# A hybrid encoder layer on one core: front steps in another order, joint level operands, 64-row products of two heads in turn

## The chip, the cores and the metric

The kernel runs on one core of one Trainium2 chip. The metric is the device time of one execution in microseconds (us), taken as the median of the runs. Engines carry the names of the profile: PE does the matmuls, DVE the vector work, ACT activations, copies and casts, POOL some vector work and the gathers by index, and SP issues most transfers. A line such as L656 is a line of the kernel's code.

## The reference, cut to what matters

One encoder layer over 512 tokens and 16 meta tokens of width 1024, in float32: a differential attention group and a bidirectional gated linear attention (GLA) group side by side, an output projection, and then a feed-forward part (PEER) in which each token picks its experts out of 16384.

```
xn = rmsnorm(h);  dq,dk,dv, gq,gk,gv,gr, zf,zb = split(xn @ w_in)
da = diff_attention(dq, dk, dv)             # 4 heads, 2 x 64 wide, values 128 wide
go = gla(gq, gk, gv, log_sigmoid gates)     # 4 heads, 64-wide keys, forward + backward
h  = h + concat(rmsnorm(da), rmsnorm(go) * silu(gr)) @ w_out
hn = rmsnorm(h)
s  = (hn @ w_q) . sub_keys                  # 8 heads x 2 halves x 128 keys
idx, gate = top 16 of the 16 x 16 sums of both halves' top 16
h  = h + sum_k gate * gelu(hn . u[idx]) * v[idx]
```

The output is the final RMSNorm of h without the meta tokens.

## The kernel before

All large products are exact to about float32: each operand is split into a rounded part (hi) and a rest (lo), and three matmuls, hi·hi (L131), lo·hi (L132) and hi·lo (L133), add up in one PSUM bank. ACT casts hi (L118 for streamed weights, L138 for other operands), and DVE or POOL subtracts to get lo (L120, L139).

The program has three parts.

**Front.** All projections, both attention groups and `w_out`. The string `ORDER` (L69) gives the order in which the code emits steps: `v`, `k`, `q` are projections of the attention group, `x` the GLA keys and queries of the second pair of heads, `u` one attention unit (16 of them: 4 heads by 4 blocks of queries), `w` one of the eight column blocks of `w_out` (`wo_pass`, `wo_first`), and `G` and `g` one step of the generator `gla_pair` for the first and second pair of heads. A GLA pair has twelve steps: seven levels, one that projects `gv` and `gr`, two for the chunk states (forward, backward), and two that finish one head each. In a level, DVE and POOL subtract prefix sums of the gates (`pre`; L672 and L673 on DVE), ACT takes exp, DVE multiplies with queries and keys (L677, L678: tile `ef`), PE multiplies 64-row operands (`pairmm`, L656: head 0 sits in rows 0 to 63, head 1 in rows 64 to 127, four chunks of 128 tokens each) and DVE writes the masked result into `AT` (L681). The last two steps make, per head and chunk, one product of `AT` with the values (L751) and two products of the queries with the states (`qx`·`S`, L753 and L754, again 64 rows).

**Middle.** The queries of PEER (`wq`, 16 blocks of 24 matmuls), the product with the keys (L953), and then the choice of the top 16 on DVE (`top16`, `topk2`: L188 to L256), which ends for the first 128 tokens with the tile `idx` (L992). `iof` (L922) and `keys` (L924) are loaded by SP. While DVE works on this, PE goes on with `u_tile`s (below).

**Experts.** For tokens 128 to 511 every expert is computed: 128 U tiles (`u_tile`: 24 matmuls of 384 columns, then gelu) and 128 V tiles (`v_tile`: 18 matmuls of 512 columns, tile weights `vhl`). U tiles 0 to 59 run alone, their results go to memory (`A_d`); from then on U and V tiles alternate. The gate weights for the V tiles are made as outer products of one-hot tiles (`oh`, L1024 and L1029 on DVE; L1060 and L1063 on PE, 96 banks of eight matmuls), which are placed among the U tiles: bank group n belongs to tile `A0 + int(n * AR)`, plus `AG` from n = `AL` on. The first 128 tokens use their chosen experts alone: POOL gathers a row of u or v per token (L264, 128 times each), DVE multiplies it with the token (L278) or adds it to the sum (L276). `pull(r)` hands out gathers in shares: `RA` per tile from tile `GS0` to 49, `RV` and `RUV` per V tile after that; a gather also waits until the tile three before is done.

The code emits in this order, and a scheduler that simulates the engines then sets the order of instructions on each engine; it may move independent work past each other.

## Time and profile before

| | us |
|---|---|
| median of three runs | 1642.83 |
| the runs | 1638.16, 1642.83, 1642.96 |
| profiled execution, its own time | 1635.18 |
| span of the profiled execution, first to last instruction | 1633.4 |
| PE busy (96% of the span) | 1561.7 |
| DVE busy (77%) | 1261.5 |
| ACT busy (44%) | 712.7 |
| POOL busy (35%) | 563.7 |
| mean granted TensorE clock, share of full | 0.985 |

The profile is of one execution, which took 7.65 us less than the median of the three runs. PE is busy in nearly all of it, so the questions to ask are where PE still waits, and where it is busy at less than its pace: on products that leave half of the array unused, or at a lower granted clock. A count behind an x is a count of records; a float32 matmul has two of them, a split one (L131 to L133) has one.

### The profile page before, as it was taken

To read this page: it belongs to the slowest core of one execution; us is meant where nothing else is said; L and a number is where in the kernel's file an instruction comes from. 1 tells how busy PE (TensorE), PEld (TensorE's weight loads), DVE (VectorE), ACT (ScalarE), POOL (GpSimd) and SP (SyncE) were. 2 spreads that over 40 slices of the span, in tenths; PEclk is the share of its full clock that TensorE was granted. 3 is DMA by queue.
4 is the path that set the end of the run, shared out by engine and by line. 5 is a ranking of instruction groups with operands and counts; after the bars stand their busy time and mean duration, and the time that the engine had idled before them with its cause. 6 is when DMAs were issued, how large, how long until landed. Compare 5 with 4: busy or idle time off the path is not lost.

```text
span 1633.4 us, 24035 instructions
## 1 busy us (share of the span) xinstructions
PE 1561.7 (96%) x8793; PEld 1382.3 (85%) x8793; DVE 1261.5 (77%) x2492; ACT 712.7 (44%) x1131; POOL 563.7 (35%) x419
## 2 busy tenths in 40 slices
PE   6999999999997789999999999999999999999997
PEld 6887886778897788989888888889999999998886
DVE  3888767655999796977467787788878887787877
ACT  5444654544332466777343333333333333333333
POOL 3445113048553330040011112265454443444442
PEclk9999999999999899999999999999999999999999
DMA  7112212233233466778999998799999999999975
GB/s 235 59 48 83 66 55 69 84 104 118 79 133 112 133 235 241 296 265 304 375 350 323 319 315 312 272 369 360 324 348 330 330 338 318 329 353 328 331 252 193
DMA packets 152358, 387.40 MB, mean 237 GB/s; under 512 B 12752, under 2 KB 71376, under 8 KB 150576
## 3 DMA queue, kind: packets, MB, share of 16 engines
q1 hardware_dynamic: 104432, 213.62, 38.0%
q0 software_dynamic: 36864, 134.23, 23.2%
q10 hardware_dynamic: 10944, 38.02, 6.2%
q8 instruction: 69, 1.13, 0.3%
q14 instruction: 49, 0.40, 0.1%
HBM read 342.56 MB, written 40.63 MB: 235 GB/s over the span
## 4 chain that ended last, share of the span: by engine, by line
PE 46%; issue 19%; DVE 15%; DMA 10%; POOL 7%; ACT 2%; SPq 1%; POOLq 0%; ACTq 0%; DVEq 0%
POOL gat L264 7%; PE bankg L131 6%; PE bankg L133 6%; PE bankg L132 6%; PE banka L1119 5%; PE banka L1122 5%; PE banka L1123 5%; DMA gat<-v,idx 4%; DMA gat<-u,idx 3%; PE bankp L1123 2%; PE bankp L1122 2%; PE bankp L1119 2%; DVE tiv L192 1%; DVE tiv L189 1%; DVE sc L190 1%
## 5 line engine op out<-in xcount | busy, mean ns | idle before, releaser
L264 POOL DMA_INDIRECT gat<-u,idx x128 | 201.6, 1575 | 531.2 <-PE bankp L1123 251.6
L118 ACT CAST hi<-raw 128x1024 fp32r<-128x1024 f32 x177 | 185.8, 1051 | 320.3 <-PE bankg L132 191.1
L131 PE MATMUL bankg<-un_hi,hi 128*128 128x384 f32 x896 | 303.4, 339 | 3.9 <-ACT act L1094 3.9
L132 PE MATMUL bankg<-un_lo,hi 128*128 128x384 f32 x896 | 302.5, 338 | 0.0
L133 PE MATMUL bankg<-un_hi,lo 128*128 128x384 f32 x896 | 302.3, 338 | 0.0
L264 POOL DMA_INDIRECT gat<-v,idx x128 | 157.7, 1232 | 206.7 <-PE bankp L1123 172.7
L120 DVE TENSOR_TENSOR lo<-raw,hi 128x1024 fp32r<-128x1024 f32 x142 | 174.0, 1227 | 56.3 <-ACT hi L118 52.4
L276 DVE SCALAR_TENSOR_TENSOR acc<-gat,sact,acc 128x1024 f32<-128x1024 f32 x128 | 164.3, 1284 | 58.1 <-DMA gat<-v,idx 55.0
L278 DVE CUSTOM_DVE_ANT_0 gat<-gat,hn 128x1024 f32<-128x1024 f32 x128 | 155.1, 1219 | 36.8 <-DMA gat<-u,idx 36.1
L139 DVE TENSOR_TENSOR vhl<-vraw,vhl 128x1024 fp32r<-128x1024 f32 x128 | 156.1, 1220 | 27.6 <-ACT vhl L138 26.5
L131 PEld LDWEIGHTS bankg<-un_hi,hi 128*128 128x128 f32 x896 | 169.6, 189 | 7.9 <-ACT act L1094 4.2
L132 PEld LDWEIGHTS bankg<-un_lo,hi 128*128 128x128 f32 x896 | 169.5, 189 | 3.3
L133 PEld LDWEIGHTS bankg<-un_hi,lo 128*128 128x128 f32 x896 | 169.6, 189 | 1.7 <-DVE lo L120 0.2
L138 ACT CAST vhl<-vraw 128x1024 fp32r<-128x1024 f32 x128 | 134.2, 1049 | 55.8 <-PE bankp L1123 34.6
L120 POOL TENSOR_TENSOR lo<-raw,hi 128x1024 fp32r<-128x1024 f32 x35 | 87.1, 2491 | 73.7 <-ACT hi L118 70.1
L1065 ACT ACTIVATE stg<-banka 128x512 f32<-128x512 f32 x96 | 96.9, 1165 | 11.4 <-PE banka L1063 11.0
L1094 ACT ACTIVATE act<-bankg 128x384 f32<-128x384 f32 x112 | 54.5, 487 | 30.2 <-PE bankg L133 20.7
L133 PE MATMUL bankp<-un_hi,lo 128*128 128x384 f32 x128 | 44.6, 348 | 21.9 <-DVE lo L120 21.9
L1024 DVE TENSOR_TENSOR oh<-iT,ioh 128x2048 f16<-128x2048 f16 x48 | 57.5, 1219 | 1.3 <-PE banka L1063 1.3
L1029 DVE TENSOR_TENSOR oh<-oh,gs 128x2048 f16<-128x2048 f16 x48 | 57.7, 1218 | 0.0
L1060 PE MATMUL banka<-oh 128*128 128x128 f16 x384 | 49.5, 221 | 8.2 <-DVE oh L1029 7.3
L1063 PE MATMUL banka<-oh 128*128 128x128 f16 x384 | 49.1, 220 | 0.0
(2287 smaller groups left out, 3775.1 us busy)
## 6 DMA issues: line engine op xcount, KB each, us to landing
raw<-uT SPq DMA_DIRECT2D x128, 512.0 KB
vraw<-v SPq DMA_DIRECT2D x128, 512.0 KB
W_d<-stg ACTq DMA_DIRECT2D x12, 2048.0 KB
wa<-W_d SPq DMA_DIRECT2D x32, 768.0 KB
A_d<-act ACTq DMA_DIRECT2D x60, 192.0 KB
wa<-A_d SPq DMA_DIRECT2D x15, 768.0 KB
raw<-wq SPq DMA_DIRECT2D x16, 512.0 KB
raw<-win_n SPq DMA_DIRECT2D x12, 512.0 KB
```

Of the source, the lines that this page charges most:

```text
L118: nc.scalar.copy(hi, raw)
L120: (eng or nc.vector).tensor_sub(lo, raw, hi.bitcast(F32))
L131: nc.tensor.matmul(o, lhsT=ah, rhs=bh, start=start, stop=False)
L132: nc.tensor.matmul(o, lhsT=ah, rhs=bl, start=False, stop=False)
L133: return nc.tensor.matmul(o, lhsT=al, rhs=bh, start=False, stop=stop)
L138: last[0] = nc.scalar.copy(hi, src).ins.name
L139: (eng or nc.vector).tensor_sub(lo, src, hi.bitcast(F32))
L264: g = nc.gpsimd.indirect_dma_start(out=r, out_offset=None, in_=src, in_offset=bass.IndirectOffsetOnAxis(ap=idx[:, hk:hk + 1], axis=0))
L276: nc.vector.scalar_tensor_tensor(acc0, r, sact[:, hk:hk + 1], acc0, op0=ALU.mult, op1=ALU.add)
L278: nc.vector.tensor_tensor_reduce(r, r, hn0, scale=1.0, scalar=0.0, op0=ALU.mult, op1=ALU.add, accum_out=sact[:, hk:hk + 1])
L1119: m0 = nc.tensor.matmul(o, lhsT=gh_[:, tc_], rhs=vh[:, dc], start=(j == 0), stop=False, skip_group_check=True)
L1122: nc.tensor.matmul(o, lhsT=gh_[:, tc_], rhs=vl[:, dc], start=False, stop=False, skip_group_check=True)
```

## The change

In the front, `ORDER` is a new string: it puts projections (`x`, `v`, `k`, `q`) between the first levels, and `u`, `q`, `k` between the last GLA steps and the first blocks of `w_out`. The GLA queries and keys of a pair lie in one tile `gqk`, and both prefix sums in one tile `pre` (`Bi`, `Fi`), so that a level takes one subtraction on DVE of 512 columns where two of 256 stood, and one multiplication of 1024 where two of 512 stood. POOL's two subtractions stay. `pairmm` takes the two heads in turn within a chunk, each head with a bank of its own. The finish of a pair makes the `AT` products of both heads first and then the `qx`·`S` products, heads in turn. `dg` of the middle and `hT` lie in other buffers. The load of `keys` stands behind the loop that makes `un_hi`, and so the code's order of the two loads on SP changes. Of the numbers, `GS0`, `RA`, `RUV`, `A0` and `AR` change: fewer gathers among the U tiles, more per V tile, and outer products from an earlier tile on. The number of PE matmuls is the same.

```diff
-GS0 = 12
+GS0 = 20
-RA = 0.3
+RA = 0.15
 RV = 0.85
-RUV = 2.92
+RUV = 3.0
-ORDER = 'GGGxGGGGGGGkGGggvgqggukugguqugguuukuvgqgukqgwuwuuuwwwuuuww'
+ORDER = 'GGxGGvGkGGGqGGGGggugkugguqguguvgkuguqgugkuguqwuwuwuwuwuwuww'
-A0 = 15
-AR = 0.48
+A0 = 11
+AR = 0.56
...
-        def pairmm(q_, k_, hh):
-            rows = slice(64 * hh, 64 * hh + 64)
-            b = bank((P, 4, P), tag=PT["pair"])
+        def pairmm(qk):
+            bs = [bank((P, 4, P), tag=PT["pair"]) for _ in range(2)]
             for c in range(4):
                 cs = slice(c * P, (c + 1) * P)
-                nc.tensor.matmul(b[:, c, :], lhsT=k_[rows, cs], rhs=q_[rows, cs], start=True, stop=True)
-            return b
+                for hh in range(2):
+                    rows = slice(64 * hh, 64 * hh + 64)
+                    nc.tensor.matmul(bs[hh][:, c, :], lhsT=qk[rows, 1, cs], rhs=qk[rows, 0, cs], start=True, stop=True)
+            return bs
...
-            nc.vector.tensor_sub(E[:, :, :, 1, :], vf[:, :, :, 1, :], fm)
-            nc.vector.tensor_sub(E[:, :, :, 0, :], bm_, vb[:, :, :, 0, :])
+            nc.vector.tensor_sub(E, fr[:, :, :, 0, :], md.to_broadcast([P, 2, nb, s]))
...
             nc.scalar.activation(ef, ef, AF.Exp, scale=1.0 / 16.0)
-            nc.vector.tensor_mul(ef[:, 0, :], ef[:, 0, :], gq[pair])
-            nc.vector.tensor_mul(ef[:, 1, :], ef[:, 1, :], gk[pair][:, :T])
-            for hh in range(2):
-                b = pairmm(ef[:, 0, :], ef[:, 1, :], hh)
+            nc.vector.tensor_mul(ef, ef, gqk[:, :, :T])
+            for hh, b in enumerate(pairmm(ef)):
                 nc.vector.copy_predicated(AT[hh], msk[:, li, None, :].to_broadcast([P, 4, P]), b)
...
+        gob = [bank((P, 4, P), tag=PT["go"]) for _ in range(2)]
+        for hh in range(2):
+            for c in range(4):
+                nc.tensor.matmul(gob[hh][:, c, :], lhsT=AT[hh][:, c, :], rhs=gv[:, c, hh * P:hh * P + P], start=(c == 0),
+                                 stop=False, skip_group_check=True)
+        for dr in (1, 0):
+            for c in range(3 + (dr == 0)):
+                cs = slice(c * P, c * P + P)
+                for hh in range(2):
+                    r = slice(64 * hh, 64 * hh + 64)
+                    nc.tensor.matmul(gob[hh][:, c, :], lhsT=qx[dr][r, cs], rhs=st[dr][r, c, :], start=False,
+                                     stop=(dr == 0 and c == 3), skip_group_check=True)
         for hh in range(2):
...
-            b = bank((P, 4, P), tag=PT["go"])
-            for c in range(4):
-                cs = slice(c * P, c * P + P)
-                nc.tensor.matmul(b[:, c, :], lhsT=AT[hh][:, c, :], rhs=gv[:, c, hc], start=True, stop=False)
-                if c < 3:
-                    nc.tensor.matmul(b[:, c, :], lhsT=qx[1][r, cs], rhs=st[1][r, c, :], start=False, stop=False)
-                nc.tensor.matmul(b[:, c, :], lhsT=qx[0][r, cs], rhs=st[0][r, c, :], start=False, stop=True)
...
-    dg = tz("dg", [P, 4, P])
+    dg = fx("dgh", [P, 4, P], "gvs")
...
-    keys = qs.tile([P, 2 * PH, NK], F32, name="keys")
-    nc.sync.dma_start(out=keys, in_=I["keys"])
...
         split(un_hi[:, k, :], un_lo[:, k, :], hk, nc.gpsimd)
+    keys = qs.tile([P, 2 * PH, NK], F32, name="keys")
+    nc.sync.dma_start(out=keys, in_=I["keys"])
```

**The products of a level on PE.** Before, with buffer numbers: the four matmuls of head 0 (one bank), then the four of head 1 (the next bank), between split matmuls of a projection.

```order
L132 MATMUL bankg_838<-lo_623,act_hi0_77 128x256
L133 MATMUL bankg_838<-hi_621,act_lo0_79 128x256
L131 MATMUL bankg_838<-hi_680,act_hi1_78 128x256
L656 MATMUL banka_718<-ef_710 128x128 x4
L656 MATMUL banka_724<-ef_710 128x128 x4
L132 MATMUL bankg_838<-lo_682,act_hi1_78 128x256
L133 MATMUL bankg_838<-hi_680,act_lo1_80 128x256
```

After, one level (now L662) of the changed program:

```order
L132 MATMUL bankg_733<-lo_599,act_hi0_77 128x256
L133 MATMUL bankg_733<-hi_597,act_lo0_79 128x256
L662 MATMUL banka_564<-ef_558 128x128
L662 MATMUL banka_565<-ef_558 128x128
L662 MATMUL banka_564<-ef_558 128x128
L662 MATMUL banka_565<-ef_558 128x128
L662 MATMUL banka_564<-ef_558 128x128
L662 MATMUL banka_565<-ef_558 128x128
L662 MATMUL banka_564<-ef_558 128x128
L662 MATMUL banka_565<-ef_558 128x128
```

Each matmul now stands beside one of the other head, in the other half of the rows. The `qx`·`S` products of the second pair stand in turn only in part, and those of the first pair still stand as seven of head 0 and seven of head 1, although the code emits them in turn: the scheduler has drawn them apart.

**The first product with the keys on PE.** Before, the end of 40 `wq` matmuls that stand between the product that makes `hrow` (L903) and the first product with the keys:

```order
L131 MATMUL banka<-hg_hi_3647,hi 128x512
L132 MATMUL banka<-hg_lo_3648,hi 128x512
L133 MATMUL banka<-hg_hi_3647,lo 128x512
L131 MATMUL banka<-hg_hi_3647,hi 128x512
L953 MATMUL bankg<-keys,pq 128x128 x4
L132 MATMUL banka<-hg_lo_3648,hi 128x512
```

After, the same place (L914 makes `hrow` out of `dgh`, L964 is the product with the keys):

```order
L914 MATMUL banka<-dgh,ones 128x512
L131 MATMUL banka<-hg_hi_3473,hi 128x512
L132 MATMUL banka<-hg_lo_3474,hi 128x512
L131 MATMUL banka<-hg_hi_3473,hi 128x512
L132 MATMUL banka<-hg_lo_3474,hi 128x512
L964 MATMUL bankg<-keys,pq 128x128 x4
L133 MATMUL banka<-hg_hi_3473,lo 128x512
```

Four `wq` matmuls stand between the two instead of 40; the later products with the keys follow at the same distance as before. On SP, `keys` now stands ahead of `iof`.

**DVE behind `idx`.** Before, five small operations of the later top-k (the choice for tokens 128 to 511), then the lo parts of the next three U tiles:

```order
L992 SCALAR_TENSOR_TENSOR idx<-sel 128x128
L220 TENSOR_SCALAR sm_row<-sm_bp 128x128
L221 TENSOR_SCALAR sm_bp<-sm_bp 128x128
L226 CAST sm_rf<-sm_row 128x128
L227 CAST sm_cf<-sm_bp 128x128
L229 SCALAR_TENSOR_TENSOR sm_t_6141<-sm_rf,sm_cf 128x128
L120 TENSOR_TENSOR lo<-raw,hi 128x1024 x3
```

After, thirteen such operations stand behind `idx`, of which these are the last three ahead of the first lo part, and what comes before the second:

```order
L239 TENSOR_TENSOR eq<-sm_cb,io16b 128x2048
L212 TENSOR_TENSOR sm_gate<-sm_gate,hrs 128x128
L227 CAST sm_cf<-sm_bp 128x128
L120 TENSOR_TENSOR lo<-raw,hi 128x1024
L231 TENSOR_SCALAR sm_bsv<-sm_rf 128x128
L243 TENSOR_TENSOR eq<-eq,tf 128x2048
L229 SCALAR_TENSOR_TENSOR sm_t_6005<-sm_rf,sm_cf 128x128
L1021 CAST gs<-gT 128x16x8
L1035 TENSOR_TENSOR oh<-iT,ioh 128x2048 x4
L245 TENSOR_TENSOR eq<-eq 128x64x16
L120 TENSOR_TENSOR lo<-raw,hi 128x1024
```

The lo parts that PE waits for moved behind top-k work and behind the first one-hot tiles. The first outer product stands behind U tile 16 instead of 19, the last ahead of tile 49 instead of 52, and the first V tile behind tile 54 instead of 57: six U tiles lie between the last outer product and the first V tile in both.

## Rows read from the trace of the kernel before

**Rows 1.** Busy time by stage: window, then engines, clock, DMA share, GB/s
```profile
0.00:200.00 200.00, 182.47 (x1291) 158.08 (x1292) 146.54 (x311) 105.11 (x210) 76.61 (x84) 0.99 0.30 96
...
460.00:565.00 105.00, 85.25 (x478) 84.71 (x478) 99.31 (x431) 32.09 (x46) 42.14 (x14) 0.90 0.39 130
565.00:797.00 232.00, 214.72 (x1699) 206.80 (x1699) 177.41 (x190) 154.33 (x183) 42.81 (x10) 0.98 0.76 273
797.00:1616.00 819.00, 817.78 (x4000) 723.86 (x3999) 645.95 (x810) 289.25 (x396) 305.50 (x245) 1.00 0.92 325
```
**Rows 2.** What PE waited for, 40 to 355: us in total, times, longest
```profile
PE bankp L471 <- DVE ss L144: 2.0, 1, 2.0
PE banka L769 <- DVE gy L765: 1.9, 1, 1.9
...
PE banka L656 <- DVE ef L678: 0.2, 1, 0.2
```
**Rows 3.** Timeline of PE at one level: start, us, operation, idle before
```profile
73.91 1.68 PE L656 MATMUL banka<-ef 64*128 64x128 f32 x16 [0.25 <-DVE ef L678]
75.52 0.38 PE L132 MATMUL bankg<-lo,act_hi 128*128 128x256 f32 x1
```
**Rows 4.** Line 656 alone, in two windows of 10 ns: records under way
```profile
74.25:74.26 0.01, 0.01 (x3) 0.01 (x2) 1.00 0.00 0
74.57:74.58 0.01, 0.01 (x4) 0.01 (x4) 1.00 0.00 0
```
**Rows 5.** Timeline of PE in the finish of one head
```profile
248.59 0.48 PE L753 MATMUL banka<-S,qx 64*128 64x128 f32 x2
...
249.65 0.48 PE L753 MATMUL banka<-S,qx 64*128 64x128 f32 x2
...
252.18 0.44 PE L538 MATMUL bankp<-ident,dy 128*128 128x128 f32 x2
```
**Rows 6.** Timeline of PE at the end of the second pair
```profile
274.17 0.63 PE L515 MATMUL banka<-ident,pr 128*128 128x128 f32 x4
274.63 0.27 PE L516 MATMUL banka<-ident,pr 128*32 128x128 f32 x1
```
**Rows 7.** Busy time by stage, behind the end of the second pair
```profile
280.00:300.00 20.00, 20.00 (x71) 13.13 (x69) 11.97 (x31) 11.41 (x39) 0.00 (x0) 0.68 0.17 53
```
**Rows 8.** What SP's queue waited for, 340 to 400
```profile
SPq L922 <- PE banka L903: 16.2, 1, 16.2
```
**Rows 9.** Timeline of PE at the first products with the keys
```profile
382.79 0.39 PE L131 MATMUL banka<-hg_hi,hi 128*128 128x512 f32 x1
383.01 1.05 PE L953 MATMUL bankg<-keys,pq 128*128 128x128 f32 x8
```
**Rows 10.** Busy time by stage, at the end of the first top-k
```profile
520.00:540.00 20.00, 0.53 (x2) 0.53 (x3) 19.93 (x109) 0.00 (x0) 1.14 (x1) 0.62 0.00 0
```
**Rows 11.** Timeline of DVE and PE behind it
```profile
536.96 0.27 DVE L992 SCALAR_TENSOR_TENSOR idx<-sel 128x128 int32<-128x128 f32 x1
...
538.14 2.41 DVE L120 TENSOR_TENSOR lo<-raw,hi 128x1024 fp32r<-128x1024 f32 x2
...
539.47 0.69 PE L133 MATMUL bankp<-un_hi,lo 128*128 128x384 f32 x1 [19.75 <-DVE lo L120]
```
**Rows 12.** What PE waited for, 460 to 800
```profile
PE bankp L133 <- DVE lo L120: 21.9, 2, 19.7
PE banka L1060 <- DVE oh L1029: 7.3, 5, 3.4
```
**Rows 13.** What DVE waited for, 540 to 800
```profile
DVE gat L278 <- DMA gat<-u,idx: 20.4, 6, 6.1
```
**Rows 14.** Timeline of POOL, 540 to 797: the first two of ten gathers
```profile
555.22 12.05 POOL L264 DMA_INDIRECT gat<-u,idx  x1 [15.91 <-PE bankg L133]
578.33 0.94 POOL L264 DMA_INDIRECT gat<-u,idx  x1 [11.07 <-PE bankp L133]
```
**Rows 15.** A group of DVE from 797 on: busy, mean ns, idle before
```profile
L278 DVE CUSTOM_DVE_ANT_0 gat<-gat,hn 128x1024 f32<-128x1024 f32 x117 | 141.6, 1219 | 16.4 <-DMA gat<-u,idx 15.7 <-issue 0.5
```

More of the change, by code (lines that the diff above doesn't have):

```diff
@@ L583, in _emit, with proj_g, proj_gqk @@
         nc.vector.tensor_mul(zT[:, w], b, rsb[:64, w])
[L585 to L586 removed]
+    def proj_g(c, meta, scale, o):
         for w, b in gemm_t(meta):
             nc.vector.scalar_tensor_tensor(o[:, w], b, scale, rsb[:, w], op0=ALU.mult, op1=ALU.mult)
[L589 to L592 removed]
+    def proj_gqk(n):
+        o = f1.tile([P, 2, TM], F32, name=f"gqk{n}")
+        proj_g(8 + n, True, 1.0, o[:, 1])
+        proj_g(10 + n, False, 0.125, o[:, 0])
+        return o
+    gqks = [proj_gqk(0)]
     rrs.append(fx("rr1", [P, TM], "rr1"))
@@ L630, in log_gate @@
         nc.vector.memset(garr[:, :, 0:1], 0.0)
-        nc.vector.tensor_sub(garr[:, :, 1:], m[:, :n].rearrange("p (c w) -> p c w", w=w),
-                             a[:, :n].rearrange("p (c w) -> p c w", w=w))
+        x, y = (v[:, :n].rearrange("p (c w) -> p c w", w=w) for v in ((m, a), (a, m))[dr])
+        nc.vector.tensor_sub(garr[:, :, 1:], x, y)
     def gla_pair(pair):
-        pre = []
+        pf = f1.tile([P, 2 * (T + 1) + P], F32, name="pre")
+        Bi, Fi = pf[:, :T], pf[:, T + 1:2 * T + 1]
+        btot = f2.tile([P, 4], F32, name="btot")
         for dr in range(2):
@@ L638, in gla_pair @@
             log_gate(dr, pair, 0, T, g)
-            pf = f1.tile([P, 4, P + 1], F32, name=f"pre{dr}")
             for c in range(4):
-                nc.vector.tensor_tensor_scan(pf[:, c, :], ones, g[:, c, :], 0.0, op0=ALU.mult, op1=ALU.add)
-            pre.append(pf)
-        Fi, Bi = pre
+                nc.vector.tensor_tensor_scan((Fi, Bi)[dr][:, c * P:c * P + P], ones[:, :P], g[:, c, 1 - dr:P + 1 - dr], 0.0,
+                                             op0=ALU.mult, op1=ALU.add)
+        Fi4, Bi4 = (v.rearrange("p (c n) -> p c n", c=4) for v in (Fi, Bi))
+        nc.vector.tensor_add(btot, Bi4[:, :, P - 1], g[:, :, P])
         gm = f2.tile([P, 1, NM + 1], F32, name="gm")
@@ L718, in gla_pair @@
                 nc.scalar.activation(em, em, AF.Exp, scale=1.0 / 16.0)
-                nc.vector.tensor_mul(em, em, gk[pair][:, None, T:].to_broadcast(mb))
+                nc.vector.tensor_mul(em, em, gqk[:, 1, None, T:].to_broadcast(mb))
                 bm2 = bank(tag=PT["state"])
@@ L802, in wo_first @@
         b = wo_pass(c, 4)
-        hc = fx(f"hT{c}", [P, T], ptag[c])
+        if c < 4:
+            if c % 2 == 0:
+                hps.append(fx(f"hTp{c}", [P, 2, T], f"gqk{c // 2}"))
+            hc = hps[-1][:, c % 2]
+        else:
+            hc = fx(f"hT{c}", [P, T], ptag[c - 4])
         nc.vector.tensor_add(hc, xr, b)
```

60 lines of the change are left out of this document (27 added, 33 removed).

## The prediction

> **What bounds the kernel now.** I read the busy time by stage first. From 797 us on PE is busy 817.78 of 819 us at full clock [rows 1]: there the kernel is as long as its matmuls, and the change leaves their number alone. From 0 to 200 us PE is busy 182.47 of 200, with a slow start in it; after that, from 40 to 355 us, the list of PE's waits has only ten entries, from 2.0 us down to 0.2, some 10 us in all [rows 2]. So PE bounds the front too, and time is to be had there only from matmuls that run below their pace, or from a clock that falls. Between 460 and 797 us PE does wait: 20 us out of 105 (85.25 busy) and 17 out of 232 (214.72 busy) [rows 1]. From 520 to 540 us PE is all but idle while DVE is busy 19.93 of 20 [rows 10], so DVE bounds this stretch, by the chain of top-k work that ends in `idx`. The same list names the two causes: 21.9 us for a lo part from DVE, 7.3 us for one-hot tiles [rows 12].
>
> **The front: products of a level.** Sixteen such groups stand in the front (seven levels and the first product, two pairs). From the first record of one to the next split matmul there pass 75.52 - 73.91 = 1.61 us for 16 records [rows 3]. A record of 128 columns takes 0.115 us from start to start (0.46 us for four [rows 6]), so 16 in a row would take 1.84 us. That it took less has its reason in the windows of line 656: two weight loads are under way while head 0 runs alone, four where its tail meets the head of the other [rows 4]. So products in different row halves do run side by side in this kernel, only here for the few at the joint. Where all eight matmuls alternate, as the order of after shows, the group should take eight double slots of 0.115 = 0.92 us and some 0.2 for entry and exit, about 1.1. Gain 0.5 us x 16 = 8 us; bounds 0 (no further overlap) and 13 (1.61 halved). I take 8, since the four loads under way are the nearest row. The Trainium skill, page "TensorEngine Tiling (Array Packing)", section "Theoretical Speedup", gives up to 2x where a dimension is at most 64; halving the whole group by it would make 12.9 us of my 8. Its section "Key Properties" adds that a change of tiling mode drains the engine. The entry and exit that I left in agree with that.
>
> DVE's joined subtraction and multiplication save instructions, but PE waited for the level's operands only 0.2 us [rows 2], so I count nothing; the levels' other work hides it, and the projections that `ORDER` puts between the first levels keep that cover. ACT's exp and POOL's subtractions are as long as before.
>
> **The front: finishing a head.** From 248.59 to 252.18 us, 3.6 us, a head makes 20 records of `AT` and `S` products, one chunk after the other, with a change from 64 to 128 rows and back in each chunk: one chunk takes 249.65 - 248.59 = 1.06 us for six records [rows 5], where six at 0.115 would take 0.69. After, all `AT` products stand first. 20 records at 0.115 are 2.3 us: 1.3 us a head, 5 us for four. With the `S` products fully in turn it would be another 4, but the order shows those of the first pair one head after the other; I take 5, bounds 2 and 9.
>
> **The front: its end.** Before, the last `g` is followed by `w` directly: PE waits 2.0 us for an attention unit and 1.9 for `gy` [rows 2], and then the clock is down: 0.68 granted from 280 to 300 us with PE busy throughout [rows 7], which is 0.32 x 20 = 6.4 us. After, a unit and a `q` projection (24 matmuls of 512 columns, 24 x 0.22 = 5.3 us by [rows 9]) stand between. That covers both waits. I count the waits, 4 us, and not the clock: further on, three units stand with no `w_out` work between them, where it may fall as well. Against it, the `gy` transposes of the first pair now have little PE work behind the `S` products, where before a longer stretch of projection stood. I price this as the same wait at the other pair, +4. Front: -8 - 5 - 4 + 4 = -13, bounds -28 and +3.
>
> **The middle: the keys.** Before, SP's queue waits 16.2 us for the `hrow` product at L922, the load of `iof`, and `keys` stands behind it [rows 8]; the first product with the keys starts at 383.01 [rows 9]. After, `keys` goes first and waits for POOL's last sum alone, and the first product stands 36 `wq` matmuls earlier: 36 x 0.22 = 8 us [rows 9]. What is queued behind on SP is `iof`, needed late, and the next `wq` weights, which came behind both anyway. DVE's chain from there to `idx` is full, so it would end 8 us earlier against PE's work. But PE waits not for `idx`: it waits for the lo part of a U tile that stands 1.2 us behind it [rows 11]. After, late top-k work that the order now has ahead of `idx`, and eight more operations between `idx` and the lo part, make 3 to 4 us each (0.27 us for a small operation, as much as a lo part, 1.2 us, for a large one [rows 11]), and the second lo part comes some 7 us after the first, of which a U tile (24 matmuls of 384 columns, 24 x 0.17 by [rows 9] scaled to the columns) covers four. Together +10 against -8: +2 for the hole of 19.75 us, bounds -8 and +6.
>
> **The middle: gathers and outer products.** The shares 0.3 for 38 tiles become 0.15 for 30, so 11 gathers among the U tiles become four. Seven of them take 7 x 1.3 us from DVE (1219 ns and a short read [rows 15]), 9 us, and of DVE's wait of 20.4 us for gathers [rows 13] some 13. PE's idle 17 us from 565 to 797 hangs mostly on DVE, and outer products from tile 16 on give DVE's one-hot tiles more room. 22 us of relief on DVE can't give PE more than the 17; I take 11, bounds 3 and 15. The work put ahead of the lo parts is then also gone from here. Six U tiles lie between the last outer product and the first V tile in both, so the way of the gate weights through memory is covered as before.
>
> **The V tiles.** Seven gathers come on top of 245, at 3.0 a tile instead of 2.92. DVE has 819 - 646 = 173 us free there, PE has none [rows 1], so 9 us more on DVE cost nothing on PE; the end of the gathers moves by one, +1 us. Middle and end: +2 - 11 + 1 = -8.
>
> **Sum.** -13 - 8 = -21 us on the profiled execution's 1635.18 us, 1614. That execution is 7.65 us below the median of the three runs, 1642.83, against which the result will be held, so the forecast is **1622 us**.
>
> **Rivals.** (1) *PE is starved where cover is short* (slower). The new order takes projections away from between later steps: behind the first pair's end, and in the stretch of three units without `w_out` work. A place like the one before costs its wait and then the clock: 4 + 6.4 = 10 us [rows 2, 7]. One wait of 4 is in my sum. With three places at the full price, 31 - 4 = +27: 1649. It decides from the third place on; two leave it about the same. For it speaks that clock and wait did come together once; against it that PE's queue is otherwise full in the front, and that the scheduler fills gaps with loose matmuls.
> (2) *The heads don't run side by side*, because the two banks or the weight loads hold each other up. Then the 8 us are gone: 1630. Against it: [rows 4].
> (3) *The gathers are only moved.* At 3.0 a tile, three gathers meet in every V tile, DMA is already at 0.92 [rows 1], and a gather on POOL can take 12.05 us or 0.94 [rows 14]. If DVE waits for them before the splits, each of the seven costs what it costs on DVE, 9 us, and I get 1631. The Trainium skill, page "SBUF — State Buffer", section "Who interferes with whom", says that a DVE operation with two SBUF inputs shuts GpSimd out for its whole length if the latter reads SBUF. By that rule the 12.05 fits the one-hot stretch, and V tiles, full of two-input operations, would suffer likewise; that POOL is busy only 305.50 of 819 us there speaks against it [rows 1].
> (4) *DVE's chain is the whole middle.* The hole shrinks by the full 8 us (10 better than my +2), the groups of a level halve (5 more): 1607.
>
> **How the numbers follow.** Forecast 0.53, rival 1 0.15, rival 2 0.11, rival 3 0.09, rival 4 0.12. 0.3% of 1642.83 is 5 us, what a measurement of this kernel can tell from no change. Rival 1 is slower (0.13, with 0.02 the same). Rivals 2 and 3 lie at -12, and spread by half their way over the line of -5: 0.14 faster, 0.06 the same. The forecast with its bounds is faster in 0.47, the same in 0.05, slower in 0.01; rival 4 is faster. That makes 0.73, 0.13 and 0.14. The range: below, both rival 4 and some of the forecast's spread, down to 1600; above, rivals 2 and 3 with their spread and the small ends of the terms, up to 1643, which leaves out rival 1 and some 0.05 more.
>
> **What would show it.** In the profile after: a level's 16 records within some 1.1 us to the next split matmul (rival 2: 1.6); the finish of a pair in about 5 us; PE's waits in the front at 10 us or less and the clock not under 0.9 behind the last `g` (rival 1: several windows near 0.7); the first product with the keys about 20 us earlier on the clock of the trace (13 of the front, 8 of its own); PE's hole behind `idx` still 18 to 22 us (rival 4: 10); DVE's wait for u gathers before the first V tile near 7 us; the V tiles with PE full again, at the same pace (rival 3: PE waits there). The prediction is wrong if PE waits over 20 us in the front, or if the first V tile starts less than 10 us earlier than at 797.

## The result: slower by 0.6%, all of it in the front

The changed kernel takes 1649.58 us (median of 11 runs, 1644.25 to 1657.75), the kernel before 1641.3 beside it. The ratio is 1.0057 with a 95% interval of 1.0037 to 1.0078, so the change costs some 9 us where 21 us of gain were forecast. One of the eleven runs of before, of 3089.65 us, is not in the ratio. The profiled execution of after takes 1652.42 us (span 1650.6) at a mean clock of 0.968, against 1635.18 and 0.985 before. These two lie 17.2 us apart, twice as far as the medians: the one of before is 6 us faster than its median, the one of after 3 us slower. What is read from the two traces below shows where the time goes, and some 8 us of it are scatter between executions.

The loss has one place. The first `w_q` matmul, with which the front ends on PE, starts at 379.7 us instead of 354.0: 25.7 us later. From there to the end it is 1650.6 - 379.7 = 1270.9 us instead of 1633.4 - 354.0 = 1279.4: 8.5 us less. The forecast for this second part was 8 less; for the front it was 13 less. The first V tile starts at 797.4 us, no earlier than before, but with three U tiles fewer ahead of it.

Busy time of after by windows of 20 us, around the ends of the two head pairs (columns as in [rows 1]):

```profile
120.00:140.00 20.00, 17.63 (x80) 11.86 (x79) 10.94 (x20) 6.17 (x11) 4.91 (x4) 0.74 0.22 67
140.00:160.00 20.00, 11.22 (x54) 8.59 (x53) 15.67 (x57) 8.72 (x22) 6.37 (x8) 0.66 0.03 5
240.00:260.00 20.00, 15.76 (x100) 12.55 (x98) 14.73 (x27) 10.96 (x24) 11.20 (x9) 0.98 0.24 72
260.00:280.00 20.00, 19.29 (x98) 15.15 (x99) 10.23 (x42) 7.43 (x21) 0.00 (x0) 0.76 0.14 42
280.00:300.00 20.00, 16.67 (x64) 11.60 (x63) 18.70 (x47) 10.87 (x27) 9.14 (x8) 0.83 0.16 45
300.00:320.00 20.00, 18.44 (x61) 10.91 (x60) 11.77 (x28) 11.11 (x35) 0.00 (x0) 0.66 0.27 66
```

Two stretches stand out, 120 to 160 and 240 to 320 us. In these six windows PE is idle for 21 us (20 less its busy time, added up), and what it does in the rest it does at a granted clock of 0.66 to 0.83 in five of them. [rows 7] was the one window of that kind before. The longest waits of PE from 40 to 380 us (line: total, times, longest):

```profile
PE banka L776 <- DVE gy L772: 10.7, 2, 8.5
PE banka L712 <- DVE ef L708: 4.4, 1, 4.4
PE banka L662 <- DVE AT L684: 3.3, 1, 3.3
```

The wait for `gy` (1.9 us in [rows 2]) is 10.7 us in two pieces. The timeline of PE at the longer one, the end of the first pair: the last product of queries and states, then nothing until DVE has the first chunk of the first head's `gy`.

```profile
139.87 1.50 PE L756 MATMUL banka<-S,qx 64*128 64x128 f32 x12
149.85 1.53 PE L776 MATMUL banka<-ident,gy 128*128 128x128 f32 x4 [8.48 <-DVE gy L772]
```

DVE is full meanwhile, but most of this is not the norm. By their durations, prefix sums of the second pair's gates (`pre` and what leads to it) and the first subtraction of its first level (`ef`) take more than half of the wait, and they stand ahead of `gy`:

```profile
141.68 1.36 DVE L645 TENSOR_TENSOR_SCAN pre<-ones,garr 128x128 f32<-128x128 f32 x4
147.80 1.28 DVE L678 TENSOR_TENSOR ef<-pre 128x512 f32<-128x512 f32 x2
149.00 1.85 DVE L772 SCALAR_TENSOR_TENSOR gy<-go,rs,gr 128x128 f32<-128x128 f32 x4
```

In the kernel before, `gy` (at 121.0 us) stands behind the same work of the second pair, 11 us behind the last product, but a projection fills PE there. The window of before:

```profile
100.00:120.00 20.00, 18.77 (x144) 17.30 (x142) 14.69 (x43) 9.33 (x22) 10.16 (x11) 1.00 0.17 44
```

The same place of after in windows of 2 us shows what comes with it:

```profile
140.00:142.00 2.00, 1.37 (x14) 1.17 (x11) 1.84 (x11) 1.97 (x5) 0.00 (x0) 1.00 0.00 0
144.00:146.00 2.00, 0.00 (x0) 0.00 (x0) 2.00 (x15) 0.50 (x2) 0.00 (x0) 0.50 0.00 0
152.00:154.00 2.00, 2.00 (x6) 1.52 (x6) 2.00 (x6) 0.42 (x1) 0.00 (x0) 0.50 0.13 22
158.00:160.00 2.00, 2.00 (x20) 1.61 (x20) 0.70 (x1) 1.23 (x2) 0.95 (x3) 1.00 0.00 0
```

PE works at full clock until 141.4 us and then waits. Inside the wait the clock goes to 0.50, which is 1.2 GHz, and it stays there after PE is busy again; between 154 and 160 us it comes back. So this wait is paid twice, as idle time and in the matmuls behind it. A low clock also stands ahead of it: from 126 to 134 us it is 0.51, behind waits of 1.5 and 0.8 us (0.79 in e13, behind the same waits).

To split the front into its parts, I added up over windows of 10 us from 40 us to the first `w_q` matmul: PE's idle time, its busy time times the missing share of the clock, and the rest, its work at full clock.

| from 40 us to the first `w_q`, us | before | after | difference |
|---|---|---|---|
| work at full clock | 297.8 | 284.8 | -13.0 |
| lost to the low clock | 6.6 | 25.6 | +19.0 |
| PE idle | 9.6 | 29.2 | +19.6 |
| together | 314.0 | 339.7 | +25.7 |

PE's work falls by the 13 us that were forecast, though not all of it by the products in turn (e6, e7 and e1 below). Three times as much is lost beside it.

Behind the front, in stages of after and in PE's waits from 355 to 820 us and DVE's from 540 to 800:

```profile
485.00:575.00 90.00, 65.55 (x373) 64.99 (x372) 90.00 (x416) 26.65 (x38) 28.32 (x12) 0.87 0.32 107
575.00:797.00 222.00, 215.81 (x1729) 209.68 (x1729) 172.19 (x180) 154.84 (x185) 11.54 (x4) 0.98 0.78 279
797.00:1634.00 837.00, 831.33 (x4078) 737.68 (x4076) 657.73 (x829) 296.19 (x407) 325.22 (x252) 1.00 0.91 325
```

```profile
PE bankp L1013 <- DVE sel L255: 24.5, 1, 24.5
PE bankg L131 <- ACT act L1105: 5.4, 1, 5.4
...
PE banka L1071 <- DVE oh L1040: 0.5, 1, 0.5
```

```profile
DVE gat L278 <- DMA gat<-u,idx: 3.6, 1, 3.6
```

The hole behind `idx` is now one wait of 24.5 us, for the transposes of `sel` that open the one-hot work, where a lo part cost 19.7 [rows 12]. PE's idle time up to the first V tile has gone from 17 us [rows 1] to 6.2 (222 less 215.81; 5.4 of it is one wait, at the last U tile ahead of the V tiles), the waits for one-hot tiles from 7.3 [rows 12] to 0.5, and DVE's wait for gathers from 20.4 [rows 13] to 3.6.

### The profile page after: what moved, and what is told of

Same layout as the page of the kernel before. It is cut to its first block, busy times and chain, and to the rows that moved or that the text cites. A ratio compares the mean times of both kernels' runs of the same rounds, so it can differ in the third digit from the quotient of the medians.

```text
span 1650.6 us, 23999 instructions
## 1 busy us (share of the span) xinstructions
PE 1564.1 (95%) x8793; PEld 1383.5 (84%) x8793; DVE 1263.9 (77%) x2466; ACT 714.5 (43%) x1131; POOL 538.1 (33%) x419
## 4 chain that ended last, share of the span: by engine, by line
PE 71%; DVE 14%; DMA 5%; issue 4%; ACT 3%; POOL 3%; SPq 1%; ACTq 0%; POOLq 0%; DVEq 0%
PE bankg L131 10%; PE bankg L132 10%; PE bankg L133 10%; PE banka L1134 7%; PE banka L1133 7%; PE banka L1130 7%; PE bankp L1134 3%; PE bankp L1130 3%; PE bankp L1133 3%; DMA gat<-u,idx 1%; POOL lo L120 1%; PE banka L662 1%; PE banka L1071 1%; PE banka L1074 1%; DVE lo L120 1%
## 5 line engine op out<-in xcount | busy, mean ns | idle before, releaser
L264 POOL DMA_INDIRECT gat<-u,idx x128 | 166.3, 1299 | 568.8 <-PE bankp L1134 251.9
L264 POOL DMA_INDIRECT gat<-v,idx x128 | 170.5, 1332 | 181.5 <-PE bankp L1134 154.0
L1071 PE MATMUL banka<-oh 128*128 128x128 f16 x384 | 48.5, 220 | 0.7 <-DVE oh L1040 0.5
L131 PE MATMUL bankg<-hi,act_hi 128*128 128x256 f32 x160 | 46.6, 291 | 2.3 <-ACT sil L605 1.7
L131 PE MATMUL bankg<-act_hi,hi 128*128 128x264 f32 (+1 forms) x144 | 48.3, 335 | 0.3 <-ACT rraw L400 0.2
```

What stands on the lines that cost most here:

```text
L131: nc.tensor.matmul(o, lhsT=ah, rhs=bh, start=start, stop=False)
L264: g = nc.gpsimd.indirect_dma_start(out=r, out_offset=None, in_=src, in_offset=bass.IndirectOffsetOnAxis(ap=idx[:, hk:hk + 1], axis=0))
```

## Experiments

Each kernel was run beside the kernel before; ratios are to it, with the 95% interval. The last columns split the front of the profiled execution as above.

| kernel | median us | ratio | first `w_q` | idle | low clock | work |
|---|---|---|---|---|---|---|
| before | 1641.3 | 1 | 354.0 | 9.6 | 6.6 | 297.8 |
| after | 1649.6 | 1.0057 (1.0037 to 1.0078) | 379.7 | 29.2 | 25.6 | 284.8 |
| e1 after, old `ORDER` | 1628.8 | 0.9915 (0.9887 to 0.9943) | 356.2 | 20.6 | 7.5 | 288.1 |
| e2 before, new `ORDER` | 1671.8 | 1.0171 (1.0133 to 1.0209) | 389.0 | 29.2 | 23.1 | 296.7 |
| e3 after, old place of `keys` | 1650.3 | 1.0048 (1.0028 to 1.0068) | 379.6 | 29.4 | 25.4 | 284.8 |
| e4 before, new numbers | 1632.6 | 0.9934 (0.9904 to 0.9964) | 354.3 | 9.7 | 7.5 | 297.2 |
| e5 after, cover at the first pair | 1623.6 | 0.9899 (0.9867 to 0.9931) | 351.1 | 18.6 | 5.7 | 286.8 |
| e6 before, levels in turn | 1636.5 | 0.9978 (0.9959 to 0.9997) | 352.9 | 8.8 | 12.8 | 291.3 |
| e7 before, finish in turn | 1637.3 | 0.998 (0.9963 to 0.9997) | 353.5 | 13.3 | 4.5 | 295.7 |
| e8 after, heads apart | 1652.1 | 1.0084 (1.0051 to 1.0118) | 373.4 | 27.6 | 16.3 | 289.6 |
| e9 after, `q` later | 1651.2 | 1.0085 (1.0058 to 1.0113) | 365.8 | 30.3 | 9.3 | 286.2 |
| e10 after, cover at both pairs | 1620.7 | 0.9881 (0.9847 to 0.9916) | 350.4 | 17.0 | 7.3 | 286.1 |
| e11 before, products and numbers | 1630.1 | 0.995 (0.9932 to 0.9969) | 356.8 | 20.3 | 7.7 | 288.8 |
| e12 after, idle filled | 1657.2 | 1.0112 (1.008 to 1.0145) | 393.3 | 22.4 | 26.0 | 305.0 |
| e13 after, idle filled by half | 1654.1 | 1.0104 (1.0072 to 1.0135) | 371.6 | 24.9 | 10.1 | 296.6 |
| e14 after, `v` later | 1644.7 | 1.0037 (1.0018 to 1.0056) | 372.2 | 31.2 | 13.4 | 287.5 |
| e15 after, `k` and `q` later | 1647.2 | 1.0054 (1.0035 to 1.0074) | 375.4 | 26.3 | 23.3 | 285.9 |

The columns on the front are of one execution; the medians are of several, and the two need not agree: the profiled execution was the fastest of six in e9 and e13 and the slowest of six in e12. The medians were taken at different times, beside a kernel before of 1638.8 to 1641.3 us, so kernels are compared here by their ratios.

### The order alone (e1, e2)

```diff
-ORDER = 'GGxGGvGkGGGqGGGGggugkugguqguguvgkuguqgugkuguqwuwuwuwuwuwuww'
+ORDER = 'GGGxGGGGGGGkGGggvgqggukugguqugguuukuvgqgukqgwuwuuuwwwuuuww'
```

e1 is after with this edit, e2 is before with its reverse.

> The changed kernel with the string ORDER of before; products in turn, joint operands, keys and numbers stay as after. Theory (the new order of steps starves PE at the ends of both head pairs and the clock falls there): the front loses the 26 us that it gained and keeps the gain of the products, w_q starts near 343 us instead of 379.7, PE's wait for gy under 4 us, the clock under 0.9 in at most two windows of 20 us between 40 and 340; time near 1615 to 1622 us. Rival (the joint operands and the finish of both heads at once make the chains longer and starve PE whatever the order is): w_q still starts at 370 or later, time 1645 or more.

> The kernel before with the string ORDER of after and nothing else. Theory (the order alone starves PE): the front is some 30 to 37 us longer than before, w_q starts at 384 to 391 instead of 354, windows near 0.7 of the clock at the ends of the pairs, time 1668 to 1678. Rival (the joint operands and the joined finish do it): the front within 8 us of before, time 1635 to 1650.

The new string alone costs 1.7%, 28 us, and e2 has the same two places as after (windows, and PE's waits for `gy` and for the operands of the state products):

```profile
140.00:160.00 20.00, 11.07 (x35) 8.46 (x36) 14.44 (x56) 7.26 (x19) 4.06 (x4) 0.57 0.01 3
260.00:280.00 20.00, 15.84 (x54) 10.92 (x52) 9.78 (x24) 9.48 (x26) 3.05 (x2) 0.64 0.13 40
```

```profile
PE banka L769 <- DVE gy L765: 8.9, 1, 8.9
PE banka L710 <- DVE ef L706: 3.6, 1, 3.6
```

So the theory holds: neither the joint operands nor the joined finish is needed for the loss, nor for the length of the wait for `gy`, since e2 has the old finish, one head after the other, and waits 8.9 us. e1 shows the other half, and a surprise. With the old order the changed kernel is 0.85% faster than before (23 us faster than after), but its front is not, against its forecast of 343 us and 1615 to 1622: the first `w_q` is at 356.2, 2 us later than before, though PE has 9.7 us less to do there. The rest came back as waits, spread over many lines, the largest of them:

```profile
PE bankg L131 <- ACT vN L784: 3.7, 2, 2.9
PE banka L662 <- DVE AT L684: 3.3, 1, 3.3
```

### Where cover stands (e5, e9, e14, e15, e10)

```diff
-ORDER = 'GGxGGvGkGGGqGGGGggugkugguqguguvgkuguqgugkuguqwuwuwuwuwuwuww'
+ORDER = 'GGxGGGGGGkGGqGGggvugkugguqguguvgkuguqgugkuguqwuwuwuwuwuwuww'
```

> The changed kernel with one edit of ORDER: v, k and q are taken out of the first pair's levels; k and q stand between the last steps of this pair and v right behind it, as the order of before had its projections there. The second pair and w_out stay as after. Theory (projections spent early leave PE without cover at a pair's end, where it waits and then runs at the low clock): PE's wait of 8.5 us for gy at 141 to 150 us goes below 3, the clock from 120 to 160 us from 0.74 and 0.66 to 0.9 or more, w_q starts 12 to 18 us earlier (362 to 368), while the second pair's end stays slow; time 1632 to 1639. Rival (the loss is spread over the levels and not at the pair's end): the front within 5 us of the changed kernel, time 1645 or more.

Three projections are moved: `v` and `k` stood among the first pair's levels and `q` ahead of its state steps; now `k` and `q` stand between its last steps and `v` behind them. The gain is 26 us, more than the 11 to 18 expected:

```profile
120.00:140.00 20.00, 19.94 (x163) 17.17 (x162) 19.60 (x44) 11.69 (x24) 5.58 (x6) 1.00 0.15 53
140.00:160.00 20.00, 19.39 (x134) 16.78 (x132) 14.39 (x20) 11.63 (x29) 9.49 (x10) 1.00 0.25 74
260.00:280.00 20.00, 16.15 (x66) 9.77 (x65) 19.12 (x46) 12.50 (x34) 8.57 (x7) 1.00 0.15 43
```

```profile
PE banka L662 <- DVE AT L684: 3.3, 1, 3.3
PE bankg L131 <- ACT sil L605: 2.4, 2, 1.7
```

The wait for `gy` at the first pair is gone, the clock is full there, and at the second pair too the clock holds better, though nothing in the order was edited there: from 220 to 300 us the windows of e5 have 1.00, 1.00, 1.00 and 0.83, where after, which gets there some 25 us later, has 0.98, 0.76, 0.83 and 0.66 from 240 to 320. The expectation had that place stay slow. Idle time in the front fell by 10.6 us and the clock's loss by 19.9.

Cover is not the only thing that e5 changed. Its `gy` stands on DVE ahead of the second pair's prefix sums (119.4 and 123.9 us), so the chain that PE waits for is also shorter; in e9 and e15 too `gy` stands ahead of them, in after, e2 and e14 behind. No run moves `gy` on DVE without moving a projection. What shows that cover counts is before against e2 and e1 against after, which all have `gy` late: with the old order PE waits 0.7 us for `gy` there in e1 and not at all in before.

I then split the edit. e9 moves `q` alone, to ahead of the two finishing steps (the expectation says between them); e14 moves `v` alone; e15 moves `k` and `q`.

> The changed kernel with one edit of ORDER, a third of that of e5: only q goes from ahead of the first pair's state steps to between its two finishing steps; v and k stay among the levels. Theory (what counts is PE work that can stand at the pair's end): q's 24 matmuls of 0.23 us are 5.5 us of cover, PE's wait for gy falls from 8.5 us to 3 to 5, less of the stretch from 120 to 160 us runs at the low clock, w_q starts 6 to 12 us earlier than at 379.7; time 1638 to 1645. Rival (v or k, not the amount of cover, made the difference in e5): w_q within 4 us of the changed kernel, time 1647 or more.

> The changed kernel with one edit of ORDER: v goes from among the first pair's levels to behind its end, as in e5; k and q stay as after. Theory A (any third of the edit of e5 leaves the rest of the end uncovered, as q alone did in e9): time 1643 to 1653. Theory B (v is what counts: its 48 split matmuls of 512 columns are the longest projection that can stand at the end): PE's wait for gy below 2 us, w_q starts 12 us earlier or more, time 1625 to 1637.

> The changed kernel with the other part of the edit of e5: k and q stand between the first pair's last steps, and v stays among the levels. Theory A (cover has to stand at all of the last four steps): about half of what e5 gains, time 1632 to 1643. Theory B (v behind the end is what counts): 1645 to 1653.

None gives more than a fifth of e5: by the ratios -3 us for `v`, -0.5 for `k` and `q` and +5 for `q`, against -26 for all three, and the intervals of the three overlap that of after. In e9 the wait for `gy` is covered beyond what was expected (1.2 us), and its profiled execution took 1639.95 us, but the median is on the rival's side. The idle time of its front is as long as in after (30.3 us): it turns up in other places, the longest at the second pair's state products (4.8 us, 4.4 in after):

```profile
PE banka L712 <- DVE ef L708: 6.4, 2, 4.8
...
PE banka L776 <- DVE gy L772: 1.2, 1, 1.2
```

e14 leaves both waits, for `gy` at the first pair and at the second pair's state products:

```profile
PE banka L776 <- DVE gy L772: 9.4, 1, 9.4
PE banka L712 <- DVE ef L708: 5.7, 1, 5.7
```

e15 covers the first pair (its wait for `gy` is 1.3 us, and the clock is 0.83 from 120 to 140 us and full behind that), but then runs dry at the second (240 to 260):

```profile
140.00:160.00 20.00, 18.64 (x146) 15.79 (x145) 19.79 (x28) 9.05 (x19) 11.84 (x12) 1.00 0.15 43
240.00:260.00 20.00, 14.77 (x52) 9.84 (x51) 7.53 (x20) 5.99 (x17) 0.98 (x1) 0.67 0.09 24
```

One reading is that it isn't a place that wants cover but a stock: a projection that is spent while PE is full anyway is missing at whichever latency comes later. With three held back, both ends are covered; with one or two, the gap moves. That reading fits the five kernels, but it is argued and not shown: the order on DVE moved as well, and why the parts add up to so little of the whole stays open.

> The kernel of e5 with the last k moved as well, from ahead of the second pair's last g to behind it, so that k and q stand between the last g and w. Theory (the same holds at the second pair's end): PE's idle time from 260 to 300 us, 6.6 us in e5, falls to 3 or less, and the window of 0.83 clock goes; time 1616 to 1620. Rival (the waits there are for attention units, which k only delays): 1622 to 1628.

```diff
-ORDER = 'GGxGGGGGGkGGqGGggvugkugguqguguvgkuguqgugkuguqwuwuwuwuwuwuww'
+ORDER = 'GGxGGGGGGkGGqGGggvugkugguqguguvgkuguqgugugkuqwuwuwuwuwuwuww'
```

e10 is the fastest kernel of this study, 0.9881 of before. Against e5 its interval overlaps, so that the last `k` gains anything is not shown. In the profile PE's idle time from 260 to 300 us falls to 1.0 us (40 less 19.26 and 19.76) and the window of 0.83 goes, as the theory had it, but the windows from 240 to 280 now have 0.85 and 0.89, and from 40 us to `w_q` only 0.7 us is gained.

### Products and operands (e6, e7, e8, e11)

e6 puts only the alternating `pairmm` into before, e7 only the finish of after; e8 takes the alternation out of after; e11 is before with both and the new numbers.

```diff
             for c in range(4):
                 cs = slice(c * P, (c + 1) * P)
-                nc.tensor.matmul(b[:, c, :], lhsT=k_[rows, cs], rhs=q_[rows, cs], start=True, stop=True)
+                for hh in range(2):
+                    rows = slice(64 * hh, 64 * hh + 64)
+                    nc.tensor.matmul(bs[hh][:, c, :], lhsT=k_[rows, cs], rhs=q_[rows, cs], start=True, stop=True)
```

> The kernel before with the level products of both heads in turn (two banks, rows 0 to 63 and 64 to 127 alternating) and nothing else. Theory one (PE bounds the front, as the prediction had it): a level's 16 records take 1.1 us instead of 1.6, w_q starts 8 us earlier, time 1631 to 1635. Theory two (what PE saves comes back as waits for DVE, ACT and POOL, since DVE is full at the first pair's levels and the chains of the generators set the pace): the records take 1.1 us all the same, PE's waits from 40 to 380 us grow by 5 us or more, w_q starts within 3 us of before, time 1638 to 1644.

> The kernel before with the finish of a pair as after (AT products of both heads first, then the products of queries and states, both heads ahead of the first norm) and nothing else. Theory one (PE bounds the front): 1.3 us a head less on PE, w_q starts 4 to 5 us earlier, time 1635 to 1638. Theory two (the first head's norm starts later, since its bank is done only with the second head's, and PE waits for gy longer): PE's waits for gy and around it grow by 3 us or more, w_q starts at 353 or later, time 1640 to 1646.

> The changed kernel with the level products of head 0 ahead of those of head 1, as before. Theory one (PE bounds the front): 0.5 us more for each of 16 groups, w_q starts 8 us later, time 1656 to 1660. Theory two (the front is set by the chains at the pairs' ends and by DVE): a group takes 1.6 us, and w_q starts within 3 us of the changed kernel, time 1647 to 1653.

> The kernel before with the level products in turn, the finish in turn and the new numbers; separate operands, ORDER and the load of keys as before. Theory (the parts add, and the joint operands and the load of keys bring nothing): the gains of e4, e6 and e7 together, some 15 us, time 1622 to 1629, and within 5 us of e1, which has the joint operands and the later load besides. Rival (the joint operands are what makes room on DVE for the products in turn): time 1632 or more.

The heads do run side by side. A level in after, and in e6, ahead of the next split matmul:

```profile
76.01 1.16 PE L662 MATMUL banka<-ef 64*128 64x128 f32 x16
77.10 0.38 PE L132 MATMUL bankg<-lo,act_hi 128*128 128x256 f32 x1
```

```profile
69.27 2.58 PE L657 MATMUL banka<-ef 64*128 64x128 f32 x16 [2.61 <-DVE AT L680]
...
76.94 1.16 PE L657 MATMUL banka<-ef 64*128 64x128 f32 x16
78.03 0.39 PE L132 MATMUL bankg<-lo,act_hi 128*128 128x256 f32 x1
```

77.10 - 76.01 = 1.09 us, as forecast (1.61 in [rows 3]). The row at 69.27 shows what becomes of it at the first pair: PE waits 2.6 us for `AT`, the masked result of the level before, because DVE is full there (19.97 of 20 us from 60 to 80). PE's work falls by 6.5 us in e6 and by 2.1 in e7; in time the ratios make it 3.6 and 3.3 us, with intervals that end just short of no change (0.9997). In their profiled executions the first `w_q` comes only 1.1 and 0.5 us earlier. The two theories on e6 both fail in part: its idle time doesn't grow (8.8 us against 9.6), but what the low clock costs does, by 6.2 us, from 70 to 80 us behind this wait (0.67) among other places. e11, with both products and the new numbers, can't be told from e4, which has the numbers alone (ratios 0.995 and 0.9934), where its forecast had 1622 to 1629 us. So PE's work shrinks as it should, and that time follows is at the edge of what these runs can tell for each product alone, and not shown for both together. e8 has 4.8 us more work than after and can't be told from it in time. The intervals of e11 and e1 overlap, so the joint operands and the rest that e1 has beyond e11 bring nothing that these runs can tell.

### The middle (e3, e4)

```diff
     iof = w1.tile([P, NK], F32, name="iof")
     nc.sync.dma_start(out=iof, in_=I["iota"].to_broadcast([P, NK]))
+    keys = qs.tile([P, 2 * PH, NK], F32, name="keys")
+    nc.sync.dma_start(out=keys, in_=I["keys"])
```

> The changed kernel with the load of keys where it stood before, ahead of the un loop. Theory (the earlier load moves DVE's whole top-k chain 8 us forward against PE's work, and PE waits for that chain): the first product with the keys comes some 30 to 40 w_q matmuls later, PE's hole behind idx grows from 24.5 us to some 32, time 1655 to 1659. Rival (the load was not what set the chain): hole and time as in the changed kernel, 1647 to 1652.

> The kernel before with GS0, RA, RUV, A0 and AR of after and nothing else. Theory (fewer gathers among the U tiles relieve DVE, and PE's waits for one-hot tiles and lo parts behind the hole go): DVE's wait for u gathers before the first V tile from 20 us to under 8, PE's waits from 565 to 797 us from 17 us to under 9, the V tiles at the old pace, time 1628 to 1636. Rival (the gathers are only moved, and the V tiles pay for them): PE waits in the V tiles, time 1639 to 1646.

e3 puts the load back, and nothing moves. SP's issues in after and in e3:

```profile
391.22 0.33 SPq L954 DMA_DIRECT2D keys<-keys  x1
399.73 0.33 SPq L933 DMA_DIRECT2D iof<-iota  x1
```

```profile
391.18 0.33 SPq L935 DMA_DIRECT2D keys<-keys  x1
399.69 0.33 SPq L933 DMA_DIRECT2D iof<-iota  x1
```

`keys` goes out 8.5 us ahead of `iof` in both. So it isn't the place of the load in the code that freed it. What did is open: the edits left are those that put tiles in other buffers, `dg` and `hT` among them, and none was tried alone. The first product with the keys does come 20.8 us behind the first `w_q` in after, e1 and e3, and 29.0 in before and e4. But from `w_q` to the end after (1270.9) and e4 (1625.7 - 354.3 = 1271.4) are alike: the earlier chain shows no more than 0.5 us in these executions.

e4, the numbers alone, has the whole gain of the middle: ratio 0.9934, DVE's wait for gathers 4.3 us, PE idle for 5.8 us between the hole and the V tiles (17 in [rows 1]). The hole itself is 26.0 us in e4, so the new numbers make it longer; after, with the earlier chain, has 24.5.

```profile
DVE gat L278 <- DMA gat<-u,idx: 4.3, 2, 3.1
```

```profile
550.00:775.00 225.00, 219.19 (x1747) 213.71 (x1746) 176.01 (x183) 156.21 (x186) 11.11 (x4) 0.98 0.76 276
```

### Filling the idle time (e12, e13)

```diff
             b = bank((P, 4, P), tag=PT["go"])
+            if hh == 0:
+                for j in range(FILL[pair]):
+                    m = nc.tensor.matmul(b, lhsT=ident, rhs=AT[1], start=True, stop=True)
```

> The changed kernel with useless float32 matmuls of 512 columns put on PE where it waits for gy: 16 at the first pair's end, 4 at the second's, written into the bank that the transposes then overwrite. They need nothing that is late and should end before gy is there (16 take some 7.3 us of the 8.5). Theory (the waits cost twice: the idle time itself, and then matmuls at the low clock): the first part stays, the second goes, since PE is not idle; the clock from 142 to 157 us stays at full (0.5 in the changed kernel), w_q starts 3 to 8 us earlier although PE has 9 us more to do, time 1641 to 1647. Rival (the clock falls for another reason, or the low clock costs nothing that isn't covered): w_q starts at 379 to 389, time 1649 to 1659.

> The kernel of e12 with half the useless matmuls: 8 at the first pair's end, 2 at the second's. In e12 sixteen took 14.0 us on PE, twice what was reckoned, and gy was late by 3.6 us for it; eight take 7.0 us of the wait of 8.5. Theory (the wait costs twice, once as idle time and once as low clock behind it): the clock from 134 to 157 us stays at full, the split matmuls from 150 to 157 us run at twice the pace, w_q starts 3 to 7 us earlier than in the changed kernel; time 1642 to 1647. Rival (the low clock behind the wait is not worth its price, or comes anyway a little later, as it did in e12 at 160 us): 1648 to 1653.

e12 was mis-sized: sixteen such matmuls take 14.0 us, not 7.3, and made `gy`'s transposes late. Its clock is 0.58 from 126 to 134 us, about as in after, then full from 134 to 158, where after has 0.85, 0.58 and 0.57; but behind a wait of 2.3 us it falls to 0.62 from 158 to 166, and over the front e12 loses as much to it as after (26.0 us). e13 has half. In its profiled execution the clock does what the theory says; the same windows of e13 and of after:

```profile
142.00:150.00 8.00, 6.03 (x18) 2.80 (x17) 8.00 (x29) 3.98 (x9) 2.95 (x3) 1.00 0.00 0
150.00:158.00 8.00, 8.00 (x52) 6.37 (x51) 3.23 (x8) 2.50 (x5) 3.48 (x4) 1.00 0.07 13
```

```profile
142.00:150.00 8.00, 0.15 (x1) 0.18 (x1) 7.97 (x34) 3.31 (x11) 3.39 (x4) 0.58 0.00 0
150.00:158.00 8.00, 7.71 (x21) 5.63 (x21) 5.16 (x14) 2.21 (x5) 2.02 (x2) 0.57 0.06 12
```

From 150 to 158 us e13 makes 52 records where after makes 21. Its first `w_q` is 8 us earlier, and that execution took 1643.71 us. But its six runs go up to 1659.05, and the median, 1654.08, is no better than after's. So in both executions the filled stretch keeps its clock; that this pays for the whole kernel is not shown: the median lies 1 us above the rival's range and 7 above the theory's.

## Why the prediction was wrong

**The products of a level**: right in size on PE (1.1 us a group, [rows 3, 4]; 6.5 us of work in e6 where 8 were forecast). **The finish**: forecast 5 us, measured 2.1 us of work in e7. Together that is 8.6 of the 13 us (9.7 by e1 against before); the rest of the fall in work came with the order, for which none was forecast. One step that failed is that from work to time: the text took PE as the bound of the front, because it waited only 10 us there [rows 2]. That was true of before, with its order. At the first pair's levels DVE is as full as PE, and a PE that is faster there waits 2.6 us for `AT` (e6). The ratios give at most 3.6 us for the levels and 3.3 for the finish, and nothing that shows for both together (e11). That the joint operands bring nothing, as the text had it, fits e11 and e1. The bound of 1.61 halved, for which the Trainium skill was named (page "TensorEngine Tiling (Array Packing)", section "Theoretical Speedup"), was not reached: 1.09 us with entry and exit.

**The end of the front** is the step that decided. It had -4 for the second pair's end and +4 for the first's, on the ground that a unit and a `q` projection, so the text, "covers both waits". Idle time grew by 19.6 us and the clock's loss by 19.0. The text priced the wait at the first pair as the same 4 us; it is 8.5, because the second pair's prefix sums stand ahead of `gy` on DVE, in before too, where a projection hid them. It counted no low clock behind it, though [rows 7] gave its price, and it had no wait at the second pair's state products (4.4 us). It looked at one place at a time; the new order had spent its projections among the levels. The bounds of -28 and +3 for the front can't be added up from those given for its terms, but +25.7 is outside either way.

**Rival 1** was this case: waits, and then the clock, at several places. Its mechanism was right. Its time of 1649 agrees with the median by luck in part: it had 27 us more for the front than the forecast, and the profiled front came out 38.7 us above the forecast (25.7 + 13), while the two profiled executions lie 8 us further apart than the medians. The argument against it, that PE's queue is otherwise full in the front, is the one that e2 refutes. **Rival 2** is out (the heads run side by side), and so is **rival 3**: PE idles 5.7 us of 837 in the V tiles of after against 1.2 of 819 before, not 9 more, and e4 keeps its gain to the end. The rule of the Trainium skill on DVE and GpSimd (page "SBUF — State Buffer", section "Who interferes with whom"), by which the V tiles would suffer, is not borne out there: a gather takes POOL 1.25 to 1.33 us on average from 797 us on in after, against 12.05 for the one of [rows 14]. Whether a gather is an operation that the rule means, no run shows. **Rival 4** is out, with a hole of 24.5 us.

**The middle**: -8 forecast, -8.5 measured, but not by its parts. The numbers alone give it (e4); the load of `keys` gives nothing in e3, and an earlier first product with the keys next to nothing. PE's idle time between the hole and the V tiles fell by the 11 us forecast, but the hole grew by 4.8 us instead of 2, and the V tiles idle 4.5 us more, where none was forecast. From `w_q` to the end PE is idle only 4 us less; the rest of the 8.5 is work at full clock and some clock, by terms that the sum does not have.

**The level of the forecast.** It added 7.65 us from the profiled execution to the median. That was sound: the execution of before that was profiled was a fast one, with a clock of 0.985, while 87 further runs of before lie between 0.975 and 0.987, and the 11 beside after have a median of 1641.3 us, 6.1 above it.

## What to carry to other kernels

Before moving independent work forward in an order, look at what it covers where it stands: work that fills a full engine covers nothing there, and is missing at the next chain of latencies. Look also at what the engine that PE waits for does meanwhile: here more than half of the wait was work of a later step, placed ahead of the result. A wait of the matmul engine should be priced with the slow matmuls behind it, and that price with a wide range: with 29 to 31 us of idle time in the front, the low clock cost 25.6 us in after, 13.4 in e14 and 9.3 in e9, each in one execution. And a saving on the bounding engine is time only until the next engine is full; read that engine's busy share in the same window before counting it.

## What was not expected of the hardware

The same kernel on the same chip varies with its clock. The six runs of e9 go from 1639.95 us at a mean granted clock of 0.978 to 1657.3 at 0.967: span times missing share of the clock rises from 36.0 to 54.6 us, 18.6, and the time by 17.4. After varies in the same way (1644.25 at 0.972, 1657.75 at 0.966). This is no mark of an order with many waits: 19 runs of before on one chip go from 1633.97 us at 0.984 to 1653.48 at 0.975. So one profiled execution can be far from the median, as that of e9 was, and a difference of a few us between two of them is not yet one between their kernels.
